# Rotary embedding on one core: which rows of a batch a partition holds

## The chip, the core and the metric

The kernel runs on one of the cores of a Trainium2 chip. A core has a matrix engine (TensorE, PE in the profile), a vector engine (VectorE, DVE), a scalar engine (ScalarE, ACT), a general engine (GpSimd, POOL) and a queue engine (SyncE, SP) that only issues transfers. They work out of an on-chip memory of 128 partitions and a small accumulator memory, PSUM. Sixteen DMA engines move data between the on-chip memory and HBM, the chip's main memory. Instructions on SP and on ACT start such transfers; each has a queue of its own (q1 is SP's, q10 ACT's in the profile).

The metric is the time of one execution on the device, in microseconds. A trace of one execution shows when each instruction and each packet of a transfer ran; its span is the time from the first recorded event to the last, and is a little shorter than the execution's own time.

## What is computed

```python
x   = randn(8, 2048, 8, 64)       # batch, sequence, heads, head width, float32
cos = randn(2048, 32); sin = randn(2048, 32)

x1, x2 = x[..., :32], x[..., 32:]
out1 = x1 * cos - x2 * sin        # cos, sin broadcast over batch and heads
out2 = x1 * sin + x2 * cos
out  = concatenate([out1, out2], axis=-1)
```

Each element of x is read once and each element of out is written once: 33.55 MB each way. For every output element there are two products and one sum.

## The kernel before

A batch is 2048 sequence positions of 512 floats. It is cut into 128 rows of R = 16 positions, 8192 floats or 32 KB each, which lie one behind the other in HBM. (In this document a "row" is such a block.) Partition q holds row q, so a whole batch is one tile `xt` of 128 x 8192 floats, 4 MB. The tables cos and sin are cut in the same way: partition q holds the 16 table entries of its 16 positions, 512 floats or 2 KB.

**Loads.** SP first reads the two tables (lines 74 and 75), then batches 0 to 4, all on its own queue (line 67). Batch 0 is read in three parts of 4, 4 and 8 positions of each row (1, 1 and 2 MB), the others whole. There are NBUF = 5 buffers, so the loads of batches 5, 6 and 7 are issued behind the work of batches 0, 1 and 2 and wait until the result of that batch has been written out and its buffer is free.

**Setup.** POOL makes two 128 x 128 matrices, `eye` and minus `eye` (`neye`), lines 80 and 81. DVE copies cos to PSUM (line 90), makes `nsin`, the negated sine table (line 91), and copies sin to PSUM (line 92).

**Work on a piece.** A batch is worked on in pieces of 4 positions, 128 x 2048 floats (`UNIT`; at the ends of the run also of 2 positions). For most pieces (kind A) POOL makes t2, the products with the sine table, in two instructions of 128 x 1024: the upper half with `sin_sb`, then the lower half with `nsin` (line 121). DVE makes t1 = x * cos (line 128) and the sum t1 + t2 (line 135), which goes back over x in the same buffer. For the first piece of batches 2, 4 and 5 (kind B) the sum is made on PE, as two products with `eye` that add up in PSUM (lines 142 and 143), and ACT copies it back (line 144). For the first piece of batches 1 and 3 (kind C) DVE makes both products (lines 128 and 147), PE adds them with `eye` or `neye` (lines 159 and 160), and ACT copies (line 164).

**Stores.** When a batch is done it is written from its buffer on ACT's queue (line 72); batch 0 goes in three parts and batch 7 in three parts, the latter on SP's queue, which has no more loads by then.

The instructions on each engine and queue run in the order in which the program gives them (`keep`).

## Time and profile before

| | us |
|---|---|
| median of 3 runs | 168.79 (168.58 to 170.59) |
| the profiled execution's own time | 170.85 |
| its span in the trace | 169.0 |
| DVE busy | 141.1 (83%) |
| POOL busy | 139.3 (82%) |
| PE busy | 49.7 |
| ACT busy | 11.4 |

The profiled execution took 2.06 us longer than the median of the runs. All times within the trace are counted from the start of the span. In the profile, L121 is line 121 of the kernel; `xt<-in_x_dram` means that the tile xt is written and x is read. A DMA is split into packets that the 16 DMA engines carry; the DMA share is the mean busy share of these 16.

The six largest stores on ACT's queue took a median of 31.6 us from issue to landing, the seven whole-batch loads 41.9 us.

### The profile page before, as it was taken

Reading aid. Unit: us, or ns where it says so; the run is one execution under the profiler, and the core shown is the slowest. Engines: PE = TensorE matmul, PEld = TensorE weight load, DVE = VectorE, ACT = ScalarE, POOL = GpSimd, SP = SyncE. Lnnn points to the kernel's source line nnn. Section 1 sums busy time; section 2 is a strip of 40 time slices with the busy share of each in tenths; the row PEclk is TensorE's granted clock in tenths of the full one; section 3 lists DMA queues with packets and bytes.
Section 4 is the critical chain, followed back from the end, with each engine's and each line's share of the span. In section 5 each row is a group of like instructions: output and inputs, shape, how many; then the busy total and the mean of one; then the engine's idle time right before and its main releaser. Section 6 shows DMA issues by size and latency. Waiting matters only on the chain.

```text
span 169.0 us, 461 instructions
## 1 busy us (share of the span) xinstructions
PE 49.7 (29%) x80; PEld 18.7 (11%) x80; DVE 141.1 (83%) x68; ACT 11.4 (7%) x11; POOL 139.3 (82%) x72
## 2 busy tenths in 40 slices
PE   0000000497309752974087609750000000000000
PEld 0000000142003311321032204210000000000000
DVE  2169799999999999999999994699789996999900
ACT  0000000032200220022002200220000000000000
POOL 2099999999999999949999479995999949999300
PEclk9999999999975997599759975997555555555555
DMA  5999999999999999999899999999999999879660
GB/s 174 405 436 465 419 431 403 406 419 450 411 473 419 442 426 419 419 442 419 380 465 405 450 403 452 395 457 395 419 434 411 457 411 457 388 337 430 277 279 25
DMA packets 3459, 67.65 MB, mean 400 GB/s; under 512 B 385, under 2 KB 385, under 8 KB 769
## 3 DMA queue, kind: packets, MB, share of 16 engines
q1 hardware_dynamic: 2160, 38.27, 53.7%
q10 hardware_dynamic: 1296, 29.36, 40.9%
q14 instruction: 3, 0.02, 0.0%
HBM read 34.08 MB, written 33.55 MB: 400 GB/s over the span
## 4 chain that ended last, share of the span: by engine, by line
DMA 48%; DVE 35%; POOL 8%; issue 2%; SPq 0%; DVEq 0%; POOLq 0%; ACTq 0%
DMA xt<-in_x_dram 28%; DMA out_dram<-xt 20%; DVE t L128 18%; DVE xt L135 16%; POOL t L121 8%; DVE t L147 1%; SPq L75 0%; SPq L74 0%; DVEq L135 0%; POOLq L121 0%; SPq L67 0%; ACTq L72 0%
## 5 line engine op out<-in xcount | busy, mean ns | idle before, releaser
L121 POOL TENSOR_TENSOR t<-xt,sin_sb 128x1024 f32<-128x1024 f32 (+1 forms) x32 | 70.5, 2204 | 17.9 <-DMA xt<-in_x_dram 17.3
L128 DVE TENSOR_TENSOR t<-xt,cos_ps 128x2048 f32<-128x2048 f32 (+1 forms) x34 | 73.4, 2166 | 4.2 <-DMA xt<-in_x_dram 3.4
L135 DVE TENSOR_TENSOR xt<-t,t 128x2048 f32<-128x2048 f32 (+1 forms) x29 | 62.2, 2144 | 12.1 <-POOL t L121 9.6
L121 POOL TENSOR_TENSOR t<-xt,nsin 128x1024 f32<-128x1024 f32 (+1 forms) x32 | 70.6, 2206 | 0.0
L142 PE MATMUL o<-t,eye 128*128 128x512 f32 x24 | 17.2, 807 | 22.9 <-DVE t L128 19.4
L159 PE MATMUL o<-t,eye 128*128 128x512 f32 x16 | 12.1, 848 | 39.7 <-DVE t L128 37.5
L143 PE MATMUL o<-t,eye 128*128 128x512 f32 x24 | 14.9, 709 | 0.0
L144 ACT COPY xt<-o 128x1024 f32<-128x1024 f32 x6 | 6.1, 1012 | 45.7 <-PE o L143 45.7
L142 PEld LDWEIGHTS o<-t,eye 128*128 128x128 f32 x24 | 5.6, 257 | 32.3 <-issue 26.4
L159 PEld LDWEIGHTS o<-t,eye 128*128 128x128 f32 x16 | 3.7, 256 | 45.1 <-POOL t L121 32.0
L143 PEld LDWEIGHTS o<-t,eye 128*128 128x128 f32 x24 | 5.7, 237 | 8.3 <-issue 6.9
L160 PE MATMUL o<-t,neye 128*128 128x512 f32 x8 | 6.3, 882 | 0.2 <-DVE t L147 0.2
L164 ACT COPY xt<-o 128x1024 f32<-128x1024 f32 x4 | 4.0, 1012 | 22.2 <-PE o L160 11.1
L147 DVE TENSOR_TENSOR t<-xt,sin_ps 128x2048 f32<-128x2048 f32 x2 | 4.6, 2280 | 0.0
L160 PE MATMUL o<-t,eye 128*128 128x512 f32 x8 | 4.1, 592 | 0.0
L164 ACT ACT_TABLE_LOAD x1 | 1.3, 1283 | 34.2 <-DVE t L147 34.2
L90 DVE COPY cos_ps<-cos_sb 128x512 f32<-128x512 f32 x1 | 0.7, 694 | 3.4 <-DMA cos_sb<-in_cos_dram 3.4
L160 PEld LDWEIGHTS o<-t,neye 128*128 128x128 f32 x8 | 2.2, 305 | 5.3 <-issue 3.7
L160 PEld LDWEIGHTS o<-t,eye 128*128 128x128 f32 x8 | 1.5, 190 | 1.9 <-issue 1.9
L92 DVE COPY sin_ps<-sin_sb 128x512 f32<-128x512 f32 x1 | 0.7, 686 | 0.0
L80 POOL MEMSET eye<- 128x128 f32 x1 | 0.2, 204 | 0.3 <-POOLq L207 0.3
L91 DVE TENSOR_SCALAR nsin<-sin_sb 128x512 f32<-128x512 f32 x1 | 0.4, 427 | 0.0
(7 smaller groups left out, 1.2 us busy)
## 6 DMA issues: line engine op xcount, KB each, us to landing
xt<-in_x_dram SPq DMA_DIRECT2D x7, 4096.0 KB, 41.9
out_dram<-xt ACTq DMA_DIRECT2D x6, 4096.0 KB, 31.6
xt<-in_x_dram SPq DMA_DIRECT2D x2, 1024.0 KB, 7.7
xt<-in_x_dram SPq DMA_DIRECT2D x1, 2048.0 KB, 13.1
out_dram<-xt ACTq DMA_DIRECT2D x1, 2048.0 KB, 25.5
out_dram<-xt SPq DMA_DIRECT2D x1, 2048.0 KB, 12.4
out_dram<-xt SPq DMA_DIRECT2D x2, 1024.0 KB, 8.8
out_dram<-xt ACTq DMA_DIRECT2D x1, 1536.0 KB, 20.4
```

The lines of the kernel that those rows point to most:

```text
L90: keep(nc.vector.tensor_copy(cos_ps, cos_sb))
L92: keep(nc.vector.tensor_copy(sin_ps, sin_sb))
L121: nc.gpsimd.tensor_mul(out=t2u[:, :, u, :].rearrange("p (r h) d -> p r h d", h=H), in0=xu[:, :, 1 - u, :].rearrange("p (r h) d -> p r h d" ...
L128: nc.vector.tensor_mul(out=t1.rearrange("p (r k d) -> p r k d", r=nr, d=Dh), in0=xk, in1=rep(cos_ps[:, r0 : r0 + nr, :], 2 * H),)
L135: keep(nc.vector.tensor_add(out=xt, in0=t1, in1=t2))
L142: nc.tensor.matmul(oc, eye, t1[:, cs], start=True, stop=False)
L143: nc.tensor.matmul(oc, eye, t2[:, cs], start=False, stop=True)
L144: keep(nc.scalar.copy(xt[:, 2 * j * C : 2 * (j + 1) * C], o))
L147: nc.vector.tensor_mul(out=t2.rearrange("p (r k d) -> p r k d", r=nr, d=Dh), in0=xk, in1=rep(sin_ps[:, r0 : r0 + nr, :], 2 * H),)
L159: nc.tensor.matmul(oc, eye, t1u[:, gs, u, :], start=True, stop=False)
L160: nc.tensor.matmul(oc, eye if u else neye, t2u[:, gs, 1 - u, :], start=False, stop=True)
L164: nc.scalar.copy(xu[:, :, u, :], o.rearrange("p (g d) -> p g d", d=Dh))
```

## The change

The 128 rows of a batch are dealt to the partitions in another order. Writing a partition's number as 8a + c, with a from 0 to 15 and c from 0 to 7, it held row 8a + c and now holds row 16c + a: neighbouring partitions within a group of eight hold rows that lie 16 rows (512 KB) apart in HBM, and the same place in neighbouring groups holds neighbouring rows. This is done for x, for out and for the tables, so the arithmetic is untouched. In the transfers the HBM side now has the shape 16 x 8 x length, while the on-chip side stays 128 x length.

The setup is changed as well. POOL makes `eye` alone. ACT makes `nsin`, the PSUM copy of sin, and `neye` from `eye`; of the three DVE instructions only the copy of cos stays.

```diff
-    xv = x.rearrange("b (q r) h d -> b q (r h d)", q=P)
-    ov = out.rearrange("b (q r) h d -> b q (r h d)", q=P)
-    cos_src = cos.rearrange("(q r) d -> q r d", q=P)
-    sin_src = sin.rearrange("(q r) d -> q r d", q=P)
+    A = 16
+    xv = x.rearrange("b (c a r) h d -> b a c (r h d)", a=A, r=R)
+    ov = out.rearrange("b (c a r) h d -> b a c (r h d)", a=A, r=R)
+    cos_src = cos.rearrange("(c a r) d -> a c (r d)", a=A, r=R)
+    sin_src = sin.rearrange("(c a r) d -> a c (r d)", a=A, r=R)
...
-            keep(nc.sync.dma_start(out=xt[:, lo : lo + n], in_=xv[b, :, lo : lo + n]))
+            keep(nc.sync.dma_start(out=xt[:, lo : lo + n], in_=xv[b, :, :, lo : lo + n]))
...
-        keep(queue.dma_start(out=ov[b, :, lo : lo + n], in_=xts[b][:, lo : lo + n]))
-    keep(nc.sync.dma_start(out=cos_sb, in_=cos_src))
-    keep(nc.sync.dma_start(out=sin_sb, in_=sin_src))
+        keep(queue.dma_start(out=ov[b, :, :, lo : lo + n], in_=xts[b][:, lo : lo + n]))
+    keep(nc.sync.dma_start(out=cos_sb.rearrange("q r d -> q (r d)"), in_=cos_src))
+    keep(nc.sync.dma_start(out=sin_sb.rearrange("q r d -> q (r d)"), in_=sin_src))
...
-    for mat, one in ((eye, 1.0), (neye, -1.0)):
-        nc.gpsimd.memset(mat, 0.0)
-        nc.gpsimd.affine_select(out=mat, in_=mat, ..., fill=one, ...)
+    nc.gpsimd.memset(eye, 0.0)
+    nc.gpsimd.affine_select(out=eye, in_=eye, ..., fill=1.0, ...)
+    keep(nc.scalar.mul(nsin, sin_sb, -1.0))
+    keep(nc.scalar.copy(sin_ps, sin_sb))
+    keep(nc.scalar.mul(neye, eye, -1.0))
     keep(nc.vector.tensor_copy(cos_ps, cos_sb))
-    keep(nc.vector.tensor_scalar_mul(nsin, sin_sb, -1.0))
-    keep(nc.vector.tensor_copy(sin_ps, sin_sb))
```

More of the change, by code (lines that the diff above doesn't have):

```diff
@@ L71, in store @@
         queue = nc.sync if b == last else nc.scalar
-        keep(queue.dma_start(out=ov[b, :, lo : lo + n], in_=xts[b][:, lo : lo + n]))
-    keep(nc.sync.dma_start(out=cos_sb, in_=cos_src))
-    keep(nc.sync.dma_start(out=sin_sb, in_=sin_src))
+        keep(queue.dma_start(out=ov[b, :, :, lo : lo + n], in_=xts[b][:, lo : lo + n]))
+    keep(nc.sync.dma_start(out=cos_sb.rearrange("q r d -> q (r d)"), in_=cos_src))
+    keep(nc.sync.dma_start(out=sin_sb.rearrange("q r d -> q (r d)"), in_=sin_src))
     for b in range(NBUF):
         load(b)
-    for mat, one in ((eye, 1.0), (neye, -1.0)):
-        nc.gpsimd.memset(mat, 0.0)
-        nc.gpsimd.affine_select(
-            out=mat,
-            in_=mat,
-            compare_op=mybir.AluOpType.not_equal,
-            fill=one,
-            base=0,
-            pattern=[[-1, P]],
-            channel_multiplier=1,
-        )
+    nc.gpsimd.memset(eye, 0.0)
+    nc.gpsimd.affine_select(
+        out=eye,
+        in_=eye,
+        compare_op=mybir.AluOpType.not_equal,
+        fill=1.0,
+        base=0,
+        pattern=[[-1, P]],
+        channel_multiplier=1,
+    )
+    keep(nc.scalar.mul(nsin, sin_sb, -1.0))
+    keep(nc.scalar.copy(sin_ps, sin_sb))
+    keep(nc.scalar.mul(neye, eye, -1.0))
     keep(nc.vector.tensor_copy(cos_ps, cos_sb))
-    keep(nc.vector.tensor_scalar_mul(nsin, sin_sb, -1.0))
-    keep(nc.vector.tensor_copy(sin_ps, sin_sb))
     def rep(a, n):
```

## The prediction, made before the changed kernel was run

> **What bounds the kernel now.** I read the profile's page first: the engines, the 40 slices, the DMA queues.

> ```profile
> span 169.0 us, 461 instructions
> ...
> PE 49.7 (29%) x80; PEld 18.7 (11%) x80; DVE 141.1 (83%) x68; ACT 11.4 (7%) x11; POOL 139.3 (82%) x72
> ...
> DMA  5999999999999999999899999999999999879660
> ...
> DMA packets 3459, 67.65 MB, mean 400 GB/s; under 512 B 385, under 2 KB 385, under 8 KB 769
> ...
> q1 hardware_dynamic: 2160, 38.27, 53.7%
> q10 hardware_dynamic: 1296, 29.36, 40.9%
> ```

> The DMA engines are busy 53.7 + 40.9 = 94.6% of the span, 0.946 x 169.0 = 159.9 us: more than DVE (141.1) or POOL (139.3). While busy they move 67.65 MB / 159.9 us = 423 GB/s, 26.4 GB/s for each of the 16. The packets tell how a DMA is dealt out. There are 24 issues; 24 x 128 data packets and 24 x 16 small ones make 3456, and 3 fetch instructions: one packet for each partition's part, and one small one for each of 16 engines. So every DMA runs on all 16 engines, eight partitions to each.

> Next, the same run by stage (the columns are the stretch, its length, busy time of each engine with its count, granted clock, DMA share, GB/s):

> ```profile
> 8.40:30.00 21.60, 0.00 (x0) 0.00 (x0) 18.95 (x11) 0.00 (x0) 21.51 (x12) 1.00 1.04 434
> 30.00:64.50 34.50, 20.16 (x32) 7.58 (x32) 33.74 (x16) 5.33 (x5) 33.82 (x16) 0.90 1.00 428
> 64.50:98.20 33.70, 19.67 (x32) 7.31 (x32) 32.94 (x15) 4.05 (x4) 27.74 (x13) 0.80 1.01 424
> 98.20:139.10 40.90, 9.82 (x16) 3.76 (x16) 34.44 (x16) 2.02 (x2) 36.54 (x16) 0.64 1.00 424
> 139.10:150.90 11.80, 0.00 (x0) 0.00 (x0) 9.87 (x6) 0.00 (x0) 11.70 (x6) 0.50 0.95 411
> 150.90:160.80 9.90, 0.00 (x0) 0.00 (x0) 9.48 (x6) 0.00 (x0) 6.89 (x5) 0.50 0.79 334
> 160.80:169.00 8.20, 0.00 (x0) 0.00 (x0) 0.00 (x0) 0.00 (x0) 0.00 (x0) 0.50 0.38 156
> ```

> From 8.4 to 139.1 us the 16 engines never rest, and the rate hardly depends on what they do: 434 GB/s where there is little but loads, 424 where loads and stores share. What limits them is therefore met by either direction alike: the DMA engine itself, or its way into the on-chip memory. The last view, the chain that ended last, and who kept SP waiting:

> ```profile
> 64.50 33.63 DMA out_dram<-xt
> ...
> 98.20 40.87 DMA xt<-in_x_dram
> ...
> 139.20 4.61 POOL t L121 x2
> ...
> 159.53 1.23 DVE xt L135
> ```
> ```profile
> SPq L67 <- DMA out_dram<-xt: 81.1, 4, 28.1
> ```

> The store of batch 2 must land (33.63 us) before the load of batch 7 is issued, that takes 40.87 us because it shares the engines, and then 21.7 us of DVE and POOL and 8.2 us of last stores follow. The compute engines have little to spare: DVE works on x from 8.44 to 160.76, 152.3 us, with 141.1 - 1.7 (setup) = 139.4 of them busy, so even free transfers would save 12.9 us at most.

> **The setup moves: nothing.** DVE loses 0.43 us (L91) and 0.69 us (L92), POOL one fill and one select (0.20 and 0.29 us); before its first piece DVE waits 3.40 us and POOL 6.84 us for x in any case, so nothing is gained.

> ```profile
> 4.02 0.43 DVE L91 TENSOR_SCALAR nsin<-sin_sb 128x512 f32<-128x512 f32 x1
> ...
> 9.70 1.25 POOL L121 TENSOR_TENSOR t<-xt,nsin 128x512 f32<-128x512 f32 x1
> ...
> 34.17 1.28 ACT L164 ACT_TABLE_LOAD   x1 [34.17 <-DVE t L147]
> ```

> ACT's operations of 128x512 aren't in the trace; its 128x1024 copy takes 1.01 us, so each is between 0 and 1.01. The table load (1.28 us) moves ahead of them. sin lands at about 1.17 + 2.8 = 3.97 us (issue, plus the time to landing in the list of issues), so nsin is there by 3.97 + 1.28 + 1.01 = 6.26 us and all three by 8.28, against first uses at 9.70 (nsin), 31.83 (sin_ps, L147) and 34.22 (neye, L160); ACT's first store is issued at 12.24. The cover is 9.70 - 6.26 = 3.4 us; without it each microsecond would delay POOL's second instruction by one. The table load that leaves 34.17 saves nothing, since ACT then waits until 39.02 for PE. SP's issues (0.33 to 0.91 us) may lengthen with the third dimension: three of them, 0 to 0.5 us each, stand ahead of the first part of x. I take 0, as loads queue for tens of microseconds behind one another, and keep +1.5 for the range. On ACT's queue nothing else is passed by a moved step.

> **The new order of rows.** Bytes, issues and packet sizes stay: each partition's part is still one unbroken 32 KB. What changes is where the engines read and write at the same moment. Until now both sides of a DMA have 128 equal entries, which may be dealt to 16 engines in any order. Now the HBM side has 16 outer entries, and the plain way to deal it is one a per engine: engine a takes partitions 8a to 8a + 7, in the order of c. All engines then step through c together: 16 adjacent rows of HBM, and on chip the same place in each group of eight.

> On the HBM side little can come of it. The best stage ran at 434 GB/s against 424 later; if all of 30 to 139.1 us ran at 434, 109 us would shrink by 2.3%, 2.5 us. A loss there is bounded by the poorest busy row, 373 GB/s (2.0 to 8.4 us, mostly 8 KB parts): 434 / 373 = 1.16, or 0.16 x 159.9 = 26 us.

> On the chip side, no row of before shows two engines at one entrance of the memory, as nothing tells which partitions an engine carries. At best it costs nothing, or it gains what the HBM side gains. At worst two engines share one engine's 26.4 GB/s whenever both load or both store, and each packet takes twice as long: + 159.9 us. If only stages with one direction suffered: 28 us of loads until 30 us double (+28), and the 9.4 MB after 139.1 (4.85 + 3.31 + 1.28 by the last three rows) move at half of 423 GB/s, 44.5 instead of 29.9 us (+14.6): 169.0 + 42.6 = 212.

> Which value? If the limit of 26.4 GB/s is the engine's own, sharing costs nothing; if it's the entrance, it costs up to double. The rate that is the same in both directions fits both. The change stakes every transfer on this and can win at most a few microseconds; I take the entrance, and half of the full price: two engines that are out of step by anything between nothing and a whole packet meet in half their time on average. 0.5 x 159.9 = 80 us; span 169.0 + 80 = 249. The profiled execution has 1.85 us outside its span and is 2.06 us over the median, so the forecast is 249 + 1.85 - 2.06 = 249 us.

> [...]

> **The rivals.** *Nothing happens* (0.19): the dealing of partitions to engines isn't what limits, or is as before, so the change doesn't do what it says. For it: every engine has the same bytes as before. 168.8 us, 165.4 to 172.2.

> *Faster* (0.17): 16 adjacent rows are kinder to HBM. The place is 30 to 139.1 us; it decides from about 434 GB/s there, when batch 7 lands 2.5 us sooner. POOL waited 2.23 us for batches 6 and 7 each and DVE 1.95 and 1.73 us for POOL, so 3.7 us of DVE's idle time can go; with the last stores slightly quicker about 4.5 us: 164 us; the bound is 168.8 - 12.9 = 155.9. Against it: engines already at one rate in all stages.

> *A mild loss* (0.14): HBM dislikes steps of 512 KB, or the engines soon fall out of step, so that one loads while the other stores. 172 to 212 us; with half of the 26 us bound, 182.

> *The forecast* (0.50): 249 us, its own range 212 to 329.

> **How the numbers follow.** Slower 0.50 + 0.14 = 0.64, same 0.19, faster 0.17; 2% (165.4 to 172.2) is about what the measurement of this kernel can tell from no change. Leaving out the faster case, 0.17, the range runs from 165 to 329; the point is that of the likeliest case, not a mean.

> **What would show it.** The packets should stay 3459. The forecast is right if the DMA share stays near full while the stage rows fall well below 424 GB/s, first of all in the load-only stage, and batch 7's load lands after 180 us; DVE and POOL would be idle for x. If the stage rows still say 424 to 434, the entrance theory is wrong, and so is the number. If they say 440 or more, the faster rival holds. If nsin is late, POOL's first wait grows beyond 8.49 us. A fall only after the first stores would speak for HBM instead.

## The result, and the profile after

The changed kernel took 223.36 us (median of 4 runs, 219.78 to 230.08) against 169.69 us (168.58 to 170.72) for the kernel before: 1.298 times as long, 95% interval 1.279 to 1.317. Some executions of a kernel come out more than 1.5% longer than its fastest one, here those of 225.9 and 230.08 us, and the ratios in this document leave them out. The forecast was slower, 249 us, with 165 to 329 for the range. The profiled execution took 225.9 us, its span is 224.1 us.

The page of the changed kernel, the lines that answer to those of before:

```profile
span 224.1 us, 459 instructions
...
PE 50.5 (23%) x80; PEld 18.0 (8%) x80; DVE 140.6 (63%) x66; ACT 12.8 (6%) x14; POOL 139.0 (62%) x70
...
DMA  5999999999999999999999999999999999998971
...
DMA packets 3458, 67.65 MB, mean 302 GB/s; under 512 B 384, under 2 KB 384, under 8 KB 768
...
q1 hardware_dynamic: 2160, 38.27, 58.9%
q10 hardware_dynamic: 1296, 29.36, 37.2%
```

The compute engines work as long as before: DVE 140.6 for 141.1 us, POOL 139.0 for 139.3. The same bytes go in the same packets (one instruction fetch fewer). But the DMA engines are now busy for 58.9 + 37.2 = 96.1% of 224.1 us, 215.4 us, where it was 159.9. That is 55.5 us more for the same work, and the span is 55.1 us longer. The whole loss is packets that take longer.

The changed kernel by stage (stretch, its length, busy time of each engine with its count, granted clock, DMA share, GB/s); the last three stretches are cut where batch 7 lands and where the last store is issued:

```profile
8.40:30.00 21.60, 0.00 (x0) 0.00 (x0) 11.79 (x7) 0.00 (x0) 12.60 (x8) 1.00 1.02 232
30.00:64.50 34.50, 10.45 (x16) 3.77 (x16) 23.58 (x11) 2.03 (x2) 19.81 (x9) 1.00 1.00 267
64.50:98.20 33.70, 12.29 (x19) 4.41 (x20) 22.37 (x11) 2.02 (x2) 23.30 (x11) 0.68 1.02 329
98.20:139.10 40.90, 18.02 (x30) 6.37 (x29) 28.71 (x13) 4.05 (x4) 27.28 (x12) 0.75 1.00 366
139.10:187.90 48.80, 9.74 (x16) 3.49 (x16) 34.77 (x16) 2.02 (x2) 36.67 (x16) 0.60 1.01 351
187.90:209.80 21.90, 0.00 (x0) 0.00 (x0) 18.64 (x10) 0.00 (x0) 18.59 (x10) 0.50 0.96 282
209.80:224.00 14.20, 0.00 (x0) 0.00 (x0) 0.03 (x1) 0.00 (x0) 0.00 (x0) 0.50 0.56 193
```

The DMA share stays near 1.00 and the rate is far below that of before: 232 for 434 GB/s while there is little but loads, then a slow recovery to 366 for 424 where loads and stores share. Batch 7 lands at 188.1 us, 49 us later than before; what follows takes 36.0 us instead of 29.9. The waits of the changed kernel (engine, line, what it waited for: us in total, times, longest):

```profile
POOL t L122 <- DMA xt<-in_x_dram: 67.3, 9, 11.5
DVE t L129 <- DMA xt<-in_x_dram: 38.4, 9, 8.9
```

The same two lines of the kernel before:

```profile
POOL t L121 <- DMA xt<-in_x_dram: 17.3, 5, 6.8
DVE t L128 <- DMA xt<-in_x_dram: 3.4, 1, 3.4
```

Both engines now starve for x. The moved setup, on ACT's timeline (start, duration):

```profile
0.73 1.28 ACT L90 ACT_TABLE_LOAD   x1 [0.73 <-PEq L208]
5.26 0.63 ACT L90 ACTIVATE nsin<-sin_sb 128x512 f32<-128x512 f32 x1 [3.25 <-DMA sin_sb<-in_sin_dram]
5.79 0.58 ACT L91 COPY sin_ps<-sin_sb 128x512 f32<-128x512 f32 x1
6.31 0.30 ACT L92 ACTIVATE neye<-eye 128x128 f32<-128x128 f32 x1
```

All three are done by 6.6 us, and POOL needs the first, `nsin`, at 13.58 us.

### The profile page after: what moved, and what is told of

The parts are those of the page before. It is cut to its first block, busy times and chain, and to the rows that moved or that the text cites. A ratio compares the mean times of both kernels' runs of the same rounds, so it can differ in the third digit from the quotient of the medians.

```text
span 224.1 us, 459 instructions
## 1 busy us (share of the span) xinstructions
PE 50.5 (23%) x80; PEld 18.0 (8%) x80; DVE 140.6 (63%) x66; ACT 12.8 (6%) x14; POOL 139.0 (62%) x70
## 2 busy tenths in 40 slices
DMA packets 3458, 67.65 MB, mean 302 GB/s; under 512 B 384, under 2 KB 384, under 8 KB 768
## 3 DMA queue, kind: packets, MB, share of 16 engines
q1 hardware_dynamic: 2160, 38.27, 58.9%
q10 hardware_dynamic: 1296, 29.36, 37.2%
## 4 chain that ended last, share of the span: by engine, by line
POOL 47%; DMA 19%; another core or an unknown queue 17%; DVE 7%; SPq 1%; issue 1%; POOLq 0%; DVEq 0%
POOL t L122 47%; DMA xt<-in_x_dram 19%; DVE xt L136 4%; DVE t L129 3%; SPq L68 1%; SPq L75 0%; SPq L76 0%; POOLq L122 0%; DVEq L136 0%
## 5 line engine op out<-in xcount | busy, mean ns | idle before, releaser
L160 PE MATMUL o<-t,eye 128*128 128x512 f32 x16 | 11.6, 816 | 65.0 <-DVE t L129 62.8
L143 PEld LDWEIGHTS o<-t,eye 128*128 128x128 f32 x24 | 5.6, 256 | 47.7 <-issue 41.6
L160 PEld LDWEIGHTS o<-t,eye 128*128 128x128 f32 x16 | 3.7, 256 | 70.5 <-issue 66.6
L144 PEld LDWEIGHTS o<-t,eye 128*128 128x128 f32 x24 | 5.2, 232 | 10.6 <-POOL t L122 5.4
L161 PEld LDWEIGHTS o<-t,eye 128*128 128x128 f32 x8 | 1.5, 190 | 1.9 <-issue 1.9
L90 ACT ACTIVATE nsin<-sin_sb 128x512 f32<-128x512 f32 x1 | 0.6, 629 | 3.2 <-DMA sin_sb<-in_sin_dram 3.2
L91 ACT COPY sin_ps<-sin_sb 128x512 f32<-128x512 f32 x1 | 0.6, 579 | 0.0
```

The lines of the kernel that those rows point to most:

```text
L90: keep(nc.scalar.mul(nsin, sin_sb, -1.0))
L143: nc.tensor.matmul(oc, eye, t1[:, cs], start=True, stop=False)
L144: nc.tensor.matmul(oc, eye, t2[:, cs], start=False, stop=True)
L160: nc.tensor.matmul(oc, eye, t1u[:, gs, u, :], start=True, stop=False)
L161: nc.tensor.matmul(oc, eye if u else neye, t2u[:, gs, 1 - u, :], start=False, stop=True)
```

## The experiments

Three explanations were open. *Entrance*: with 16 outer entries of 8 on the HBM side (16 x 8 for short: 16 groups of 8 partitions), each DMA engine takes eight neighbouring partitions, and two engines meet at one entrance of the on-chip memory. *HBM order*: the 512 KB steps within an engine, or the adjacent rows that 16 engines read together, are bad for HBM. *Setup*: the work moved to ACT is late.

### The parts of the change, and other deals of the same rows

**The setup alone.** The kernel before with the new setup and the old rows:

```diff
-    for mat, one in ((eye, 1.0), (neye, -1.0)):
...
+    keep(nc.scalar.mul(nsin, sin_sb, -1.0))
+    keep(nc.scalar.copy(sin_ps, sin_sb))
+    keep(nc.scalar.mul(neye, eye, -1.0))
```

> Kernel before, with only the setup moved (POOL makes eye alone; ACT makes nsin, the PSUM copy of sin, and neye). Theory 'entrance' (two engines meet at one entrance of the on-chip memory because 16 outer entries of 8 neighbouring partitions are dealt out whole): the setup is worth nothing, 169 us, ratio 0.99 to 1.01. Rival 'HBM order' (the 512 KB steps in HBM cost the time): also 169. Rival 'setup' (the setup on ACT is late): some of the 54 us would show here, above 172.

168.77 us (164.17 to 169.26) against 168.86 us (167.38 to 170.95) on the same chip (medians). The setup costs nothing; one run of four was faster by more than 3 us, so a small gain is neither shown nor excluded.

**The rows alone.** The changed kernel with the old setup.

> The changed kernel with the old setup (POOL makes eye and neye, DVE makes nsin and the copies). 'Entrance' and 'HBM order' alike: the rows carry it all, 218 to 226 us. 'Setup': clearly below 220.

230.57 us (227.65 to 245.92), 1.357 times the kernel before (1.345 to 1.369). The rows carry the whole loss. All four runs lie above the 218 to 226 us that were expected; the repeat of the changed kernel further down is spread as widely.

**32 outer entries of 4.** The rows are dealt just as far apart, and one number differs:

```diff
-    A = 16
+    A = 32
```

> The changed kernel with 32 outer entries of 4 instead of 16 of 8: partition 4a + c holds row 32c + a. Steps in HBM grow to 1 MB, and the rows of a batch are dealt out just as far apart. 'Entrance': groups of four partitions can be dealt to the engines as before the change, no two engines meet, so the load-only stage is back near 430 GB/s and the time near 169 us (167 to 173). 'HBM order': steps twice as long cost as much or more, 220 us or above.

167.49 us, 0.994 times the kernel before (0.988 to 1.000). By stage:

```profile
8.40:30.00 21.60, 0.00 (x0) 0.00 (x0) 17.38 (x10) 0.00 (x0) 19.83 (x11) 1.00 1.02 426
30.00:98.20 68.20, 38.44 (x64) 14.32 (x64) 66.78 (x30) 8.10 (x8) 64.18 (x29) 0.85 1.01 431
```

The full rate is back, 426 GB/s in the load-only stage, with steps of 1 MB in HBM instead of 512 KB. That the step in HBM costs the time doesn't fit this; the next run tests the order in HBM with the shape kept.

**16 outer entries of 8, but near rows.** Partition 8a + c holds row 8a + 7 - c. Each engine's eight rows are one unbroken 256 KB, taken from the end; the minus keeps the 16 x 8 shape, as 8a + c would be one run of 128 equal steps.

```diff
-    xv = x.rearrange("b (c a r) h d -> b a c (r h d)", a=A, r=R)
+    xr = x.rearrange("b (a c r) h d -> b a c (r h d)", a=A, r=R)
...
-... in_=xv[b, :, :, lo : lo + n]
+... in_=back(xr[b, :, :, lo : lo + n], 1)      # back: the same entries, last one first
```

> The changed kernel with 16 outer entries of 8 as in the change, but the rows of HBM stay near: partition 8a + c holds row 8a + 7 - c, so each engine reads one unbroken 256 KB, backwards by rows. 'Entrance': the dealing of 16 entries of 8 is unchanged, so the time stays near 220 us (210 to 230) and the load-only stage near 230 GB/s. 'HBM order': back to 169 to 175 us, load-only stage above 400 GB/s.

229.94 us, 1.344 times before (1.327 to 1.360).

```profile
8.40:30.00 21.60, 0.00 (x0) 0.00 (x0) 12.29 (x8) 0.00 (x0) 14.58 (x9) 1.00 1.05 246
30.00:98.20 68.20, 26.02 (x41) 9.12 (x41) 50.62 (x23) 5.06 (x5) 46.43 (x21) 0.82 0.99 296
```

246 GB/s with the rows of HBM next to one another: the loss goes with the shape 16 x 8 and not with the distance, and *HBM order* falls.

**64 outer entries of 2.**

> The changed kernel with 64 outer entries of 2: partition 2a + c holds row 64c + a, the setup on ACT as in the change. 'Entrance': as with 32 entries of 4, no two engines meet, 166 to 171 us. If rows of HBM that are read side by side were worth anything, it would be below 166.

170.26 us against 168.73 (medians; six runs from 166.9 to 172.15 against eleven from 166.59 to 170.92):

```profile
8.40:30.00 21.60, 0.00 (x0) 0.00 (x0) 17.60 (x10) 0.00 (x0) 20.01 (x11) 1.00 1.03 428
```

The full rate is kept with steps of 2 MB, and no gain shows either.

### One direction at a time

Loads in one deal, stores in the other: first the loads in 16 x 8 and the stores in 32 x 4 (the edit shown), then the other way round. The output rows then lie in other places than in the reference.

```diff
-    ov = out.rearrange("b (c a r) h d -> b a c (r h d)", a=A, r=R)
+    ov = out.rearrange("b (c a r) h d -> b a c (r h d)", a=2 * A, r=R)
```

> The changed kernel with only the loads (x and the tables) in 16 outer entries of 8; the stores go out in 32 entries of 4, so rows of the output land in other places than they should. 'Entrance' in both directions: the load-only stage stays near 230 GB/s and the mixed stages rise above the 329 to 366 GB/s of the changed kernel; time between 180 and 215 us. Rival 'writes only' (only writing into the on-chip memory suffers): no better than the change, 218 to 226 us.

> The other way round: loads in 32 entries of 4, only the stores in 16 entries of 8 (again rows of the output land elsewhere). 'Entrance' in both directions: load-only stage near 430 GB/s, mixed stages below 424, and the last stores slower, 175 to 205 us. Rival 'writes only': 167 to 172 us.

Only the loads in 16 x 8: 214.64 us (207.31 to 223.32) against 170.84 (165.17 to 173.0), medians. Only the stores in 16 x 8: 198.38 us, 1.185 times before (1.148 to 1.222). First the run with only the loads dealt so, then the one with only the stores; its last row holds nothing but stores:

```profile
8.40:30.00 21.60, 0.00 (x0) 0.00 (x0) 11.79 (x7) 0.00 (x0) 13.39 (x8) 1.00 1.02 234
64.50:139.10 74.60, 31.72 (x50) 11.36 (x50) 54.57 (x25) 6.07 (x6) 54.19 (x24) 0.71 1.01 359
```
```profile
8.40:30.00 21.60, 0.00 (x0) 0.00 (x0) 17.26 (x10) 0.00 (x0) 19.83 (x11) 1.00 1.02 427
64.50:139.10 74.60, 30.72 (x48) 11.12 (x48) 62.96 (x28) 6.07 (x6) 61.60 (x28) 0.72 1.00 380
175.00:190.00 15.00, 0.00 (x0) 0.00 (x0) 0.00 (x0) 0.00 (x0) 0.00 (x0) 0.50 0.72 210
```

The store row has a DMA share of 0.72, so its 210 GB/s are 292 for a full share; before, a stretch of stores alone had 334 at 0.79, or 423. Both directions suffer, so "writes only" falls. For the loads alone it was also expected that the mixed stages rise above those of the changed kernel: 359 GB/s from 64.5 to 139.1 us is hardly more than its 349 (the mean of 329 and 366 by their lengths). Fastest run against fastest run on this chip, the loads alone cost 207.31 - 165.17 = 42.1 us, the stores alone 195.14 - 165.17 = 30.0, and both at once (the next run) 222.36 - 165.17 = 57.2: the costs don't add.

**The change again**, on the chip of these two:

> The changed kernel itself, beside e5 and e6 on the same chip: 218 to 231 us by every theory. It also tells whether the 230.6 us of the rows alone were the setup or only the spread between runs: above 226 would say spread.

226.77 us (222.36 to 243.73), 1.351 times before (1.306 to 1.396), so 230 us with the old setup is within the spread. Its profiled execution has a span of 223.7 us, and its first five stages have 238, 259, 312, 366 and 367 GB/s, for 232, 267, 329, 366 and 351 above.

### The entrance by itself

**Stages of plain transfers.** No rotation: two DMAs of 32 KB per partition in each stage, and a small copy that marks when each has landed. Only shape and number of partitions differ. This kernel and the two after it ran once each.

```python
load(32, 4); load(16, 8); load(16, 4); load(8, 4); load(8, 8); load(8, 16)     # outer, inner
store(0, 32, 4); store(2, 16, 8); store(4, 8, 4); store(6, 8, 8)
```

> No rotation at all: stages of plain transfers, one after the other, two DMAs of 32 KB per partition in each; the output is whatever lies in the tiles. Loads with outer x inner = 32 x 4, 16 x 8, 16 x 4 (64 partitions), 8 x 4 (32 partitions), 8 x 8 (64 partitions), 8 x 16, then stores 32 x 4, 16 x 8, 8 x 4, 8 x 8. [...] The deciding pair is 8 x 4 against 8 x 8: the same 8 engines, the same order in HBM, 32 or 64 partitions. Rival 'engine': an engine has a rate of its own and the dealing costs something else, for example long walks in HBM; then 8 x 8 runs at the rate of 8 x 4 (215). Rival 'writes only': the stores run at 430, 430, 215 and 215. [...]

By stage, in that order (stretch, length, busy time of DVE and POOL, clock, DMA share, GB/s). In the sixth row the first store already runs beside the second load, and its rate is too high for that reason:

```profile
14.00:31.00 17.00, 4.09 (x2) 0.00 (x0) 1.00 1.00 430
32.30:72.50 40.20, 0.25 (x2) 0.00 (x0) 1.00 1.00 209
72.70:92.30 19.60, 0.23 (x2) 0.00 (x0) 1.00 0.95 201
92.50:101.90 9.40, 0.22 (x2) 0.00 (x0) 1.00 0.56 223
102.10:142.00 39.90, 0.17 (x2) 0.00 (x0) 1.00 0.50 105
142.10:221.50 79.40, 0.23 (x2) 0.00 (x0) 1.00 0.56 132
221.70:240.70 19.00, 0.21 (x2) 0.00 (x0) 1.00 1.03 385
240.90:278.20 37.30, 0.20 (x2) 0.00 (x0) 1.00 0.85 211
278.40:289.70 11.30, 0.24 (x2) 0.00 (x0) 1.00 0.51 162
289.90:322.50 32.60, 0.17 (x2) 0.00 (x0) 1.00 0.44 110
```

The DMA share of 0.44 to 0.56 in the 8-entry stages says that 8 of the 16 engines work: an engine takes whole outer entries. The deciding pair is the fourth and fifth row: *entrance* can have 8 x 8 slower than 8 x 4, 'engine' can't. By that share, the same 8 engines load 223 GB/s into 32 partitions and 105 GB/s into 64. More partitions, half the rate: in the first case every engine has four partitions, in the second eight. If engine a takes outer entry a and all go through their entries together, the engines of 8 x 4 are 4 to 28 partitions apart at any moment, and 223 GB/s shows no loss; those of 8 x 8 are 8 to 56 apart, and of the new distances 32 alone gives each of the eight a partner, engine a + 4 to engine a. These are the pairs in what follows. (The traces don't name the partitions of an engine; the pairs are an estimate from these two rates.) Half of the first row's 430 GB/s is 215 and a quarter 108: loads of 16 x 8, 16 x 4 and 8 x 4 came to 209, 201 and 223, those of 8 x 8 to 105, and the first load of 8 x 16 landed 39.8 us after the last of 8 x 8, 4.19 MB at 105 GB/s. The stores of 16 x 8 and 8 x 8 fall in the same way, to 211 and 110, but the other two came out below the loads of their shape as well: 385 for 430 with 32 x 4, and 162 for 223 with 8 x 4. So the deciding pair is less sharp for stores, 162 against 110, and why is open.

**In step or not.** Two engines of a pair are in step when they are at the same place of their eight partitions at the same moment. Four loads of 8 x 8, then a small load that gives the lower four engines four packets more, then the same four loads; at the end loads and stores of 16 x 8 side by side.

```python
keep(nc.sync.dma_start(out=extra[64:80, :], in_=hbm(x, 4, 4, 4)))   # 4 outer entries of 4
```

> Plain transfers again (no rotation; the output is whatever lies in the tiles). First four loads of 8 outer entries of 8 on 64 partitions, which took 20 us each; then a small load of 4 outer entries of 4, which gives four of the eight engines (the lower half) four packets to carry into other partitions (64 to 79), and behind it the same four loads; then two loads and two stores of 16 x 8 side by side on two queues. Theory 'in step': two engines that share entrances are slow only while both are at the same one; four packets of delay put one of each pair at the other entrance for good, so the first four loads land 20 us apart and the last four about 10 us apart. Rival 'whatever the moment': the pairs share a fixed rate, and the last four also land 20 us apart. For the loads beside stores: 16.8 MB between 39 us (432 GB/s, directions never meet and engines alternate) and 78 us (216 GB/s, all in step); 'in step' expects less than 70.

```profile
40.00:86.00 46.00, 0.31 (x2) 0.00 (x0) 1.00 0.51 111
88.00:103.00 15.00, 0.15 (x1) 0.00 (x0) 1.00 0.51 210
106.00:140.00 34.00, 0.15 (x1) 0.00 (x0) 1.00 0.99 209
```

The same loads by the same eight engines run at 111 GB/s in step and at 210 half a DMA out of step: the engines pay only while they meet. But this lasted for one load. The expected 10 us apart was missed; the last four loads landed 14.6, 17.0, 20.1 and 18.8 us after one another. From 104 us on, the final 16 x 8 load also ran on the other eight engines, in step among themselves, and all 16 engines together got 209 GB/s, where 210 + 105 would be due if pairs were independent. The next run tests this. The loads beside stores at the end started one by one and not together, so the time that was foreseen for them can't be read; from 140 to 194 us the rate was 272 GB/s, between the two bounds, of which 432 GB/s is 16 packets of 32 KB in 1.213 us, their median in the kernel before.

**Pairs in step hold up the rest.** Loads of 16 x 8 throughout: four in step; four with the four pairs of the lower half of the partitions out of step; four with all eight pairs out of step. The last row ends before the one store is issued.

```python
for stage in range(3):
    if stage == 1: more(96, 4)                  # 4 entries of 4: four packets to engines 0 to 3
    if stage == 2: more(0, 12); more(48, 8)     # four to engines 0 to 11, four to engines 0 to 7
    for i in range(4): load(i, 16, 8)
```

> Plain loads of 4 MB in 16 outer entries of 8 (no rotation; the output is whatever lies in the tiles; one plain store at the end). Four of them in step; then a small load gives engines 0 to 3 four packets more, and four loads follow (pairs of the lower half of the partitions half a DMA out of step, those of the upper half still in step); then two small loads (four packets to engines 0 to 11, four to engines 0 to 7) put the pairs of the upper half out of step too, and four loads follow. In step, the rate is 209 GB/s. Theory 'in step, pair by pair': the second four run at about 324 GB/s (216 and 108 for the halves), the last four at 430. Theory 'in step, and a pair in step holds up the rest' (drawn from the run before, where eight engines out of step fell from 214 to about 107 GB/s when the other eight began to load in step): the second four stay near 210 to 230, the last four reach 400 or more. Rival 'a ceiling of the dealing': all of them stay near 210.

```profile
40.00:88.00 48.00, 0.31 (x2) 0.00 (x0) 1.00 0.99 208
108.00:186.00 78.00, 0.46 (x3) 0.00 (x0) 1.00 0.99 208
207.00:215.40 8.40, 0.00 (x0) 0.00 (x0) 1.00 1.02 437
```

208 GB/s with all pairs in step, still 208 with four of the eight out of step, and 437 when all are, once the small loads are through at about 205 us. The very deal of the change, with its 512 KB steps in HBM, runs at full rate as long as no two engines meet, and "a ceiling of the dealing" falls with it.

One rival for the middle row is that the four pairs had fallen back into step. The packets of this trace say no: in all four loads four engines end 10 us after the other twelve, half a load behind (at 125 us for 115, at 145 for 135). And yet every one of the 496 packets of 32 KB that started from 108 to 186 us took 2.31 to 2.57 us, as in the first four loads (2.38 to 2.57), where those from 206 to 215 us took 1.21 to 1.27. Engines that met nobody were as slow as those that met. The run has four pairs in step; how few are enough it doesn't show.

A version that beats both kernels did not come out of this: 32 x 4 is level with the kernel before, and the setup on ACT too.

## Why the prediction came out as it did

- *What bounds the kernel* was right: the compute engines did the same work, and the whole difference is in the time that packets took.
- *The setup costs nothing* was right: `nsin` at 5.9 us against the bound of 6.26, and 168.77 for 168.86 us by itself. The sign that was named for a late `nsin`, POOL's first piece after 8.49 us, came without that cause: POOL began at 12.37 us, after 11.07 us of waiting for x. The issues on SP did lengthen, to 0.54 us at the least for 0.33; the first load of x was issued at 2.07 for 1.65 us, within the 1.5 us kept for it.
- *The HBM side can bring little* was right, and less than little: steps of 1 and 2 MB cost nothing here (426 and 428 GB/s in the load-only stage), and loads with the 512 KB steps of the change reached 437 GB/s out of step. No loss from the step shows in these runs.
- *Engine a takes partitions 8a to 8a + 7, and two engines meet at one entrance* was right as far as a trace can tell that doesn't name an engine's partitions: it is borne out by the 32 x 4 deal (426 GB/s in the load-only stage for 232), the 8 x 4 against 8 x 8 stages (223 and 105), and the recovery out of step (111 to 210, and 208 to 437). That the place where they meet is an entrance of the on-chip memory is the author's reading of these rates; no trace shows the place.
- *The size* was off: half of the full price, 0.5 x 159.9 = 80 us, measured 55.5 us, or 0.35 of it. The step that failed is that the engines of a pair are out of step by anything from nothing to a packet on average, at all times. In the load-only stage they pay nearly all (434 / 232 = 1.87 times); where loads and stores alternate they pay from 428 / 267 = 1.60 times down to 424 / 366 = 1.16. That the whole came as near to a half as 0.35 is luck: nothing in the prediction gave this mix.
- What restores the rate in the mixed stages is open. The packets say where it is lost: a 32 KB packet of a load took 2.21 us (median) until 30 us, then 2.04, 1.88 and 1.52 in the next three stages, while one of a store took 1.28 and 1.24 in the last two of them, close to the 1.21 of both before. That the engines of a pair drift apart there would fit the last experiment. But the 16 engines ended the load of batch 1 within 4.6 us and that of batch 7 within 14.1 us in this trace, and each of them within 2.7 to 4.2 us in the trace of the repeat, whose rate recovers alike; so a growing distance alone isn't the reason. Nor does a run show whether one packet out of step is enough, as the prediction had it: the experiments used four.
- *Pairs pay one by one* is implied by that average and was wrong too: with four of eight pairs in step all 16 engines stayed at 208 GB/s.
- *The price if only one-way stages suffered*, 42.6 us, had the wrong stages: the end cost 36.0 - 29.9 = 6.1 us, not 14.6, and the mixed stages were not free.
- *The full price*, 169.0 + 159.9 = 329 us, the top of the range, has every packet take twice as long. Plain loads in step do, 430 to 209 GB/s. No run shows it for the whole kernel, which mixes loads and stores: 0.35 of the 159.9 us was paid.
- The signs named in advance came: stages below 424 GB/s at a full DMA share, the load-only stage first, batch 7 after 180 us (188.1), DVE and POOL idle for x.

## What to carry to other kernels

Look at the outermost dimension of both sides of a DMA, not only at bytes and row lengths: a 128-partition tile whose HBM side has 16 outer entries is, by these runs, dealt to the engines in runs of eight partitions and may load at half rate (209 GB/s in the plain loads), while 32 entries of 4 move the same kind of permutation at full rate (430). The sign in a profile is a DMA share near 1 with GB/s well below what the kernel reaches elsewhere, worst here where transfers went one way: 232 GB/s at a share of 1.02 with little but loads, 366 at 1.00 with loads and stores. A permutation that HBM doesn't ask for is not worth that risk: no order of rows tried here was clearly faster than the plain one.

## What the runs showed of the hardware beyond the question

A DMA whose HBM side has three dimensions took its queue's engine longer to issue here: the loads of x 0.57 us (median) in place of 0.38.
